# One landing for every transfer in the planner of a hybrid encoder block

## The chip, the cores and the metric

The kernel runs on one core of a Trainium2 chip. The metric is the device time of one execution in microseconds (us). A core has five engines that each work through their own list of instructions in order: TensorE (PE) for matmuls, VectorE (DVE), ScalarE (ACT), GpSimd (POOL) and SyncE (SP), which here only issues transfers. Transfers are also issued by GpSimd and, a few, by ScalarE. All of them are carried by the core's 16 DMA engines.

## The reference

One layer on 256 tokens of width 2048, float32, batch 1:

```python
x = x + 0.5 * swiglu(rms_norm(x, ffn1_norm[l]), ffn1_w_up[l], ffn1_w_down[l])
h = rms_norm(x, mix_norm[l])
proj = h @ w_in[l]
...
merged = g[:, :, 0, :] * (y_a @ w_branch_a[l]) + g[:, :, 1, :] * (y_b @ w_branch_b[l])
x = x + merged @ w_out[l]
x = x + cross_attention(rms_norm(x, xattn_norm[l]), rms_norm(mem, mem_norm[l]),
                        xattn_wq[l], xattn_wkv[l], xattn_wo[l])
x = x + 0.5 * swiglu(rms_norm(x, ffn2_norm[l]), ffn2_w_up[l], ffn2_w_down[l])
return rms_norm(x, final_norm)
```

`swiglu` is `(silu(gate) * up) @ w_down` with an inner width of 5632. `y_a` comes from a gated linear recurrence in chunks, `y_b` from a convolution and a scanned recurrence. Nearly all the work is the product of 256 tokens with weights that are each used once, so each weight is loaded, prepared and multiplied.

## The kernel before

**Stages.** First FFN (about 0 to 660 us), the mixer with its two recurrences, the cross attention (together to about 1745 us), second FFN, final norm. Weights come in pieces of 128x2048 float32, 1 MB each, and TensorE uses one after the other.

**Splitting.** Every product is computed from two parts of each operand: a high part in TensorE's fast float32 form, and what is left. For a weight piece `raw`, ScalarE writes the high part (`h<-raw`) and VectorE the rest (`l<-raw,h`). TensorE then does h times the input's high part (`xh`), h times its rest (`xl`), and l times its high part. So a weight passes through a load, ScalarE, VectorE and TensorE, and each waits for the one before.

**FFNs.** The up projection runs in 11 groups g of 8 pieces. A "fast" piece does a block product with seven products in place of eight; for that VectorE forms differences of weight blocks (`td<-raw`), which are split in turn (`h<-td`, `tl<-td,h`). At the end of a group VectorE and ScalarE take the finished accumulators from PSUM (`ev<-acc`), form the activation, TensorE transposes it (`acc<-vt,ev`), and it is split (`hidop`). Pieces of the down projection (`wd`) come behind each group, two and later four, and their results are added to the tokens (`x<-acc,x`). In the first FFN half of these down pieces are loaded twice: a GpSimd transfer adds the second load to the negated high part (`l<-own`), in place of VectorE's subtraction.

**Made sums.** For 56 pieces of the second FFN the differences are formed ahead, in the middle: GpSimd loads a piece (`made<-wu`), VectorE subtracts four times (`made<-made`), GpSimd stores the result to DRAM (`kept<-made`). In the second FFN SP loads it (`td<-kept`) beside three quarters of the piece itself.

**What sets the order.** The program is not written in the order in which it runs. Every operation is recorded (`record`), priced in microseconds (`price`, L254), and a planner (`arrange`, L291) plays the whole program through: at each step an engine takes, among the operations that are ready, the one that is due first, where due times are counted back from TensorE's. This is done twice. `emit` (L435) then writes each engine's instructions in the order found; so all matmuls, splits and transfers show L465. Semaphores keep the order correct, whatever the true durations are.

For a transfer `price` gives `op.moved`, 2.9 us a MB (5.2 for an accumulating one), and `op.lands`, the time from its last byte to the moment when it can be used. `arrange` lines transfers up behind one another (`dma`), adds the landing to each (`op.end`), and does not issue a further one while more than `BACKLOG` = 3 us are outstanding. `op.lands` enters in two places: in `op.spent`, from which the due times of all earlier operations follow, and in `op.end`, when whatever uses the transfer becomes ready. Buffers (`big`: 9, and 4 more in the FFNs) are given out in the same pass.

Of the kernel before, what the change touches and what calls it, by code (L numbers as in the profile page):

```python
# [176 lines left out]


LAG = {"PE": 0.24, "DVE": 0.15, "ACT": 0.16, "POOL": 0.16, "SP": 0.1}
AHEAD, BACKLOG, STICK = 30, 3, 8  # L180
TABLES = {ACT.Silu, ACT.Sigmoid, ACT.Sqrt, ACT.Exp, ACT.Gelu_apprx_tanh}


class Flow:
# [69 lines left out]
    def price(self, op, method, args, kw, outs):  # L254
        q = op.queue.name
        n = outs[0].cells.size if outs else 0
        if method == "dma_start":
            n = n or args[1].cells.size
            op.moved = n * 512 / 2 ** 20 * (5.2 if "accum_op" in kw else 2.9)
            op.busy = 0.9 if q == "POOL" else 0.06  # L260
            op.lands = 1.9 if q != "POOL" else 3.2 if "accum_op" in kw else 4.6 if op.tiles - {args[0].tile} == set() else 5.8
        elif method == "transpose":
            op.busy += 0.099
        elif q == "PE":
            op.busy += n / 2400 + 0.0137 if not op.turn else 0.021 if n <= 32 else 0.07 + n * 1.05e-3
        elif q == "DVE":
            n = max(n, kw["in_"].cells.size) if method == "tensor_reduce" else n
            per = {"reciprocal": 6.2, "tensor_tensor_scan": 2.2}.get(method, 1.042)
            op.busy = n * per / 1000 + 0.07
        elif q == "ACT":  # L270
            op.busy = n * 0.838e-3 + 0.095 + (0.1 if "accum_out" in kw else 0)
            op.table = args[2] if args[2] in TABLES else None
        else:
            op.busy = 1.0
# [16 lines left out]
    def arrange(self):  # L291
# [2 lines left out]
        ops = self.ops  # L294
        for op in ops:
            op.after = [a for a in getattr(op, "extra", ())]
            op.spent = op.busy + LAG[op.queue.name] + (op.moved + op.lands if op.moved else 0)
        for op in ops:
            op.waits = len(op.deps)
            for d in op.deps:  # L300
# [20 lines left out]
        dma = reached = 0.0  # L321
# [6 lines left out]
        def enter(op):  # L328
            if op.nominal > reached + AHEAD:
                heappush(later[op.queue.name], (op.nominal, op.i, op))  # L330
            else:
                insort(cand[op.queue.name], op, key=lambda o: (o.due, o.i))
# [8 lines left out]
        while events:  # L341
            t, e = heappop(events)
            if free[e] > t + 1e-9:
                continue
            while later[e] and later[e][0][0] <= reached + AHEAD:
                enter(heappop(later[e])[2])
            best, soon = None, 1e18
            for op in cand[e]:
                if best is not None and (not last or best.turn or op.due - STICK > best.due):
                    break  # L350
                if best is not None and not op.turn:
                    continue
                r = op.ready
                if op.moved:
                    r = max(r, dma - BACKLOG)
                if r <= t + 1e-9:
                    for ring in {x.ring for x in op.takes}:
                        fit = ring.fit(op, self)
                        r = max(r, fit[-1][0] if fit else 1e18)
                if r <= t + 1e-9:  # L360
                    best = op
                else:
                    soon = min(soon, r)
            if best is None:
                if soon < 1e17:
                    heappush(events, (soon, e))
                continue
            op = best
            cand[e].remove(op)
            op.start = t  # L370
            sequence.append(op)
            busy = op.busy
            if op.table is not None and op.table != table:
                table = op.table
                busy += 1.3
            if e == "PE":
                busy += 0.1 * (op.turn != last)
                last = op.turn
            free[e] = t + busy
            op.end = t + busy + LAG[e]  # L380
            if op.moved:
                dma = max(dma, t + busy) + op.moved
                op.end = dma + op.lands
            woken = {e}
            if e == "PE" and op.nominal > reached:
                reached = op.nominal
                woken.update(names)
            for ring in {x.ring for x in op.takes}:
                fit = ring.fit(op, self)
                for x in op.takes:  # L390
                    if x.ring is ring:
                        f = fit.pop(0)
                        ring.take(op, f)
                        x.place = f[1]
                        scope = ring.places[f[1]][0].scope
                        if scope is not None:
                            self.opened = max(self.opened, scope)
                            live[scope] += 1
                        if f[2] is not None:
                            for u in f[2].users:  # L400
                                if u is not op:
                                    u.extra.append(op)
                woken.update(names)
            if op.scope is not None:
                live[op.scope] -= 1
            for x in op.tiles:
                x.left -= 1
                x.ends = max(x.ends, op.end)
                if not x.left:
                    x.ring.free.append((x.ends, x.place, x))  # L410
                    if x.ring.places[x.place][0].scope is not None:
                        live[x.ring.places[x.place][0].scope] -= 1
                    woken.update(names)
            for s in op.after:
                kind = s.deps[op]
                if kind is None:
                    r = t
                elif s.queue is op.queue and not op.moved:
                    r = t + busy + (0.1 if kind and e in ("DVE", "ACT") else 0)
                else:  # L420
                    r = op.end
                s.ready = max(s.ready, r)
                s.waits -= 1
                if not s.waits:
                    enter(s)
                    woken.add(s.queue.name)
            for n in woken:
                heappush(events, (max(t, free[n]), n))
            done += 1
# [1231 lines left out]
```

## Time and profile before

| | us |
|---|---|
| median of 3 runs | 2434.31 (2431.85 to 2438.36) |
| profiled execution | 2435.0 |
| its span | 2433.2 |
| TensorE busy | 2412.0 |
| VectorE busy | 2071.1 |
| ScalarE busy | 1417.8 |
| DMA | 662.84 MB, mean 272 GB/s |

The granted TensorE clock is 0.999 of full speed on average. The span is the time from the first to the last instruction in the profile, and the execution's time lies around it. In the rows `out<-in` names the tiles written and read, with their shapes; a wait is booked with what ended it.

### The profile page before, as it was taken

Reading aid. Unit: us, or ns where it says so; the run is one execution under the profiler, and the core shown is the slowest. Engines: PE = TensorE matmul, PEld = TensorE weight load, DVE = VectorE, ACT = ScalarE, POOL = GpSimd, SP = SyncE. Lnnn points to the kernel's source line nnn. Section 1 sums busy time; section 2 is a strip of 40 time slices with the busy share of each in tenths; the row PEclk is TensorE's granted clock in tenths of the full one; section 3 lists DMA queues with packets and bytes.
Section 4 is the critical chain, followed back from the end, with each engine's and each line's share of the span. In section 5 each row is a group of like instructions: output and inputs, shape, how many; then the busy total and the mean of one; then the engine's idle time right before and its main releaser. Section 6 shows DMA issues by size and latency. Waiting matters only on the chain. (4 is left out here: it accounts for less than half of the span.)

```text
span 2433.2 us, 30931 instructions
## 1 busy us (share of the span) xinstructions
PE 2412.0 (99%) x12130; PEld 2008.5 (83%) x12130; DVE 2071.1 (85%) x2232; ACT 1417.8 (58%) x1410; POOL 83.0 (3%) x142
## 2 busy tenths in 40 slices
PE   9999999999999999999999999999999999999998
PEld 8888888888888888888888888888888788888886
DVE  8999999999955778888877877867899999999994
ACT  8556666666654444476434644545676666666663
POOL 0000000000000000000000000000000000000000
PEclk9999999999999999999999999999999999999999
DMA  8567878787835687978988888876898766776783
GB/s 305 187 238 245 266 250 260 258 248 252 279 122 191 255 298 267 355 287 331 345 328 311 336 313 320 318 295 232 329 374 304 260 248 254 253 254 257 259 302 113
DMA packets 98355, 662.84 MB, mean 272 GB/s; under 512 B 10912, under 2 KB 11168, under 8 KB 24992
## 3 DMA queue, kind: packets, MB, share of 16 engines
q1 hardware_dynamic: 77904, 517.11, 56.9%
q0 software_dynamic: 19584, 142.62, 18.0%
q8 instruction: 95, 1.56, 0.2%
q10 hardware_dynamic: 720, 1.13, 0.1%
q14 instruction: 52, 0.43, 0.0%
HBM read 574.83 MB, written 60.82 MB: 261 GB/s over the span
## 5 line engine op out<-in xcount | busy, mean ns | idle before, releaser
L465 ACT ACTIVATE h<-raw 128x2048 fp32r<-128x2048 f32 (+2 forms) x428 | 732.2, 1714 | 508.6 <-PE acc L465 132.6
L465 DVE TENSOR_TENSOR l<-raw,h 128x2048 fp32r<-128x2048 f32 (+2 forms) x428 | 870.7, 2038 | 177.4 <-ACT h L465 80.0
L465 PE MATMUL acc<-h,xh 128*128 128x512 f32 x1244 | 469.9, 390 | 0.9 <-ACT h L465 0.7
L465 PE MATMUL acc<-h,xl 128*128 128x512 f32 x1244 | 449.4, 390 | 0.0
L465 PE MATMUL acc<-h,hidop 128*128 128x512 f32 x1408 | 442.2, 391 | 1.1 <-ACT ev L465 1.1
L465 PE MATMUL acc<-h,ops 128*128 128x512 f32 x1664 | 412.4, 391 | 1.3 <-DVE gate L465 1.2
L465 ACT ACTIVATE h<-td 128x1024 fp32r<-128x1024 f32 (+1 forms) x248 | 307.8, 1249 | 171.2 <-DVE td L465 131.8
L465 PE MATMUL acc<-ops,h 128*128 128x512 f32 x1152 | 388.6, 397 | 1.2 <-ACT h L465 1.2
L465 DVE TENSOR_TENSOR tl<-td,h 128x1024 fp32r<-128x1024 f32 (+1 forms) x248 | 359.2, 1460 | 10.1 <-ACT h L465 7.9
L465 PEld LDWEIGHTS acc<-h,ops 128*128 128x128 f32 x1664 | 310.0, 188 | 65.6 <-DVE gate L465 1.5
L465 PEld LDWEIGHTS acc<-h,hidop 128*128 128x128 f32 x1408 | 262.6, 188 | 56.1 <-ACT ev L465 2.5
L465 PEld LDWEIGHTS acc<-h,xh 128*128 128x128 f32 x1244 | 232.5, 188 | 52.4 <-ACT h L465 3.1
L465 PEld LDWEIGHTS acc<-h,xl 128*128 128x128 f32 x1244 | 233.4, 188 | 48.6
L465 PE MATMUL acc<-ops,l 128*128 128x256 f32 x1152 | 270.1, 281 | 0.0
L465 PE MATMUL acc<-l,hidop 128*128 128x512 f32 x704 | 265.7, 389 | 0.0
L465 PEld LDWEIGHTS acc<-ops,h 128*128 128x128 f32 x1152 | 202.8, 188 | 32.8 <-ACT h L465 1.4
L465 PEld LDWEIGHTS acc<-ops,l 128*128 128x128 f32 x1152 | 211.4, 188 | 19.9
L465 PE MATMUL acc<-l,ops 128*128 128x512 f32 x832 | 222.6, 389 | 0.0
L465 PE MATMUL acc<-tl,xh 128*128 128x512 f32 x608 | 189.3, 392 | 3.3 <-DVE tl L465 3.2
L465 PE MATMUL acc<-l,xh 128*128 128x512 f32 x636 | 187.6, 390 | 0.0
L465 PEld LDWEIGHTS acc<-l,ops 128*128 128x128 f32 x832 | 155.5, 188 | 32.1
L465 DVE TENSOR_TENSOR made<-made 128x512 f32<-128x512 f32 x224 | 153.5, 689 | 13.0 <-DMA made<-wu 8.7
(172 smaller groups left out, 1916.8 us busy)
## 6 DMA issues: line engine op xcount, KB each, us to landing
raw<-wu SPq DMA_DIRECT2D x108, 1024.0 KB, 7.1
raw<-wd SPq DMA_DIRECT2D x72, 1024.0 KB, 6.4
made<-wu POOLq DMA_DIRECT2D x56, 1024.0 KB, 5.9
kept<-made POOLq DMA_DIRECT2D x56, 1024.0 KB, 6.4
td<-kept SPq DMA_DIRECT2D x56, 1024.0 KB, 6.7
raw<-wu SPq DMA_DIRECT2D x56, 768.0 KB, 5.6
raw<-win SPq DMA_DIRECT2D x40, 1024.0 KB, 4.9
raw<-wg SPq DMA_DIRECT2D x32, 1024.0 KB, 6.8
```

Of the source, the lines that this page charges most:

```text
L465: getattr(op.queue.real, method)(*map(real, args), **{k: real(v) for k, v in kw.items()})
```

## The change

In place of four landings, one for SP's and ScalarE's queues (1.9), and three for GpSimd's (3.2 for an accumulating load, 4.6 for a load, 5.8 for a store), the planner uses 3.5 us for every transfer.

```diff
-AHEAD, BACKLOG, STICK = 30, 3, 8
+AHEAD, BACKLOG, STICK, LANDS = 30, 3, 8, 3.5
...
             op.moved = n * 512 / 2 ** 20 * (5.2 if "accum_op" in kw else 2.9)
             op.busy = 0.9 if q == "POOL" else 0.06
-            op.lands = 1.9 if q != "POOL" else 3.2 if "accum_op" in kw else 4.6 if op.tiles - {args[0].tile} == set() else 5.8
...
-            op.spent = op.busy + LAG[op.queue.name] + (op.moved + op.lands if op.moved else 0)
+            op.spent = op.busy + LAG[op.queue.name] + (op.moved + LANDS if op.moved else 0)
...
                 dma = max(dma, t + busy) + op.moved
-                op.end = dma + op.lands
+                op.end = dma + LANDS
```

No operation is added or removed. The order changes on all five engines; three places of it follow. The line is L465 before and L464 after, since one line of the program is gone.

VectorE at the end of a group of the first FFN (the fourth or a later group; `td` are differences of up weights, `tl` their rest parts, `l<-raw,h` of 128x2048 those of down weights, `ev` the accumulators taken from PSUM). Before:

```order
L465 TENSOR_TENSOR td<-raw 128x1024
L465 TENSOR_TENSOR l<-raw,h 128x1536
L465 TENSOR_TENSOR tl<-td,h 128x1024
L465 TENSOR_TENSOR td<-raw,td 128x512
L465 TENSOR_TENSOR tl<-td,h 128x1024
L465 TENSOR_TENSOR td<-raw,td 128x512
L465 TENSOR_TENSOR l<-raw,h 128x2048
L465 TENSOR_TENSOR tl<-td,h 128x1024
L465 TENSOR_TENSOR l<-raw,h 128x2048
L465 TENSOR_TENSOR ev<-acc,ev 128x512 x5
```

After, from the same td on:

```order
L464 TENSOR_TENSOR td<-raw 128x1024
L464 TENSOR_TENSOR tl<-td,h 128x1024
L464 TENSOR_TENSOR td<-raw,td 128x512
L464 TENSOR_TENSOR l<-raw,h 128x1536
L464 TENSOR_TENSOR td<-raw,td 128x512
L464 TENSOR_TENSOR tl<-td,h 128x1024 x2
L464 TENSOR_TENSOR ev<-acc,ev 128x512 x2
L464 TENSOR_TENSOR l<-raw,h 128x2048
L464 TENSOR_TENSOR ev<-acc,ev 128x512 x2
L464 TENSOR_TENSOR l<-raw,h 128x2048
L464 TENSOR_TENSOR ev<-acc,ev 128x512
```

The last tl of the group moves ahead of the first split of down weights, and two of the five ev move ahead of it too.

VectorE in the middle of a late group of the second FFN, where a `tl` of 128x2048 belongs to a piece whose differences were stored before and one of 128x1024 to half of a piece whose differences are formed here. Before:

```order
L465 TENSOR_TENSOR l<-raw,h 128x1536
L465 TENSOR_TENSOR tl<-td,h 128x2048
L465 TENSOR_TENSOR tl<-td,h 128x1024
L465 TENSOR_TENSOR tl<-td,h 128x2048
L465 TENSOR_TENSOR l<-raw,h 128x1536
```

After:

```order
L464 TENSOR_TENSOR l<-raw,h 128x1536
L464 TENSOR_TENSOR tl<-td,h 128x1024
L464 TENSOR_TENSOR tl<-td,h 128x2048
L464 TENSOR_TENSOR l<-raw,h 128x1536
L464 TENSOR_TENSOR tl<-td,h 128x2048
```

The half `tl` moves ahead of the first whole one, and the second whole one behind a split of `raw`.

ScalarE at the end of a late group of the second FFN, where `h<-raw` of 128x2048 splits down weights and `ev<-acc` takes the first accumulator. Before:

```order
L465 ACTIVATE h<-td 128x1024
L465 ACTIVATE h<-raw 128x2048 x3
L465 ACTIVATE ev<-acc 128x512
L465 ACTIVATE h<-raw 128x2048
L465 ACTIVATE h<-raw 128x1536
L465 ACTIVATE ev<-ev,rtok 128x512
```

After:

```order
L464 ACTIVATE h<-td 128x1024
L464 ACTIVATE h<-raw 128x2048 x2
L464 ACTIVATE ev<-acc 128x512
L464 ACTIVATE h<-raw 128x2048 x2
L464 ACTIVATE ev<-ev,rtok 128x512
L464 ACTIVATE h<-raw 128x1536
```

`ev<-acc` moves ahead of the third split of down weights.

## The prediction

> **What bounds the kernel now.** I read the page's first part, then TensorE's own waits, then busy time by stretch, and last the places where TensorE stands still. The page's busy times and its span:
>
> ```profile
> span 2433.2 us, 30931 instructions
> PE 2412.0 (99%) x12130; PEld 2008.5 (83%) x12130; DVE 2071.1 (85%) x2232; ACT 1417.8 (58%) x1410; POOL 83.0 (3%) x142
> ```
>
> TensorE (PE) works 2412.0 of 2433.2 us. The 21.2 us that are left are all that any order can win. Where they lie, from TensorE's waits over the whole span, and the end of the chain of waits:
>
> ```profile
> PE acc L465 <- DVE tl L465: 3.2, 6, 0.9
> PE acc L465 <- ACT h L465: 1.9, 3, 1.2
> PE acc L465 <- ACT xg L465: 1.3, 1, 1.3
> PE acc L465 <- DVE gate L465: 1.2, 1, 1.2
> PE acc L465 <- ACT ev L465: 1.1, 2, 0.6
> PE warm L465 <- DVE ones L465: 1.1, 1, 1.1
> PE acc L465 <- DVE sum L465: 0.4, 1, 0.4
> PE acc L465 <- DVE hidop L465: 0.4, 1, 0.4
> PE acc L465 <- ACT vf L465: 0.3, 1, 0.3
> 2337.19 85.97 PE acc L465 x382
> ```
>
> The columns are the total, the number of waits and the longest. They sum to 10.9 us; 1.1 of it is the start, so 9.8 us are waits inside. The last matmul ends at 2337.19 + 85.97 = 2423.2, and the remaining 10.0 us are the final norm and the stores, which no order of loads shortens. No TensorE wait names a DMA: weights are late for ScalarE and VectorE, hardly ever for TensorE.
>
> The second engine decides how much disorder is forgiven. Busy time by stretch (TensorE, its weight loads, VectorE (DVE), ScalarE (ACT), GpSimd; clock; DMA share; GB/s), the first of the span, two of the first FFN, one of the middle and two of the second FFN:
>
> ```profile
> 0.00:60.00 60.00, 58.95 (x268) 50.01 (x269) 50.31 (x79) 51.50 (x86) 0.20 (x4) 1.00 0.81 304
> 240.00:300.00 60.00, 60.00 (x270) 49.72 (x269) 57.04 (x59) 41.86 (x34) 2.57 (x3) 1.00 0.80 255
> 300.00:360.00 60.00, 60.00 (x271) 49.76 (x270) 56.29 (x58) 40.38 (x33) 2.61 (x3) 1.00 0.79 249
> 1140.00:1200.00 60.00, 60.00 (x266) 49.71 (x265) 47.90 (x54) 28.86 (x30) 4.82 (x9) 1.00 0.97 350
> 1980.00:2040.00 60.00, 60.00 (x269) 49.43 (x268) 59.37 (x52) 37.38 (x30) 0.00 (x0) 1.00 0.67 254
> 2160.00:2220.00 60.00, 58.83 (x263) 48.14 (x262) 56.98 (x50) 35.89 (x29) 0.00 (x0) 1.00 0.69 250
> ```
>
> In both FFNs VectorE has only 0.6 to 3.7 us to spare in 60; in the middle it has 12. So an order that makes VectorE stand still costs time in the FFNs first.
>
> **Which landing is nearer.** The change moves no work; it gives the planner other landings. For a transfer of 1 MB it adds 2.9 us of moving to the landing (5.2 where it accumulates): before 4.8 for the SP queue, 7.5 for a GpSimd load, 8.7 for a store to DRAM, 8.4 for an accumulating load; after it 6.4, 6.4, 6.4 and 8.7. The page has the medians from issue to landing (last column):
>
> ```profile
> raw<-wu SPq DMA_DIRECT2D x108, 1024.0 KB, 7.1
> raw<-wd SPq DMA_DIRECT2D x72, 1024.0 KB, 6.4
> made<-wu POOLq DMA_DIRECT2D x56, 1024.0 KB, 5.9
> kept<-made POOLq DMA_DIRECT2D x56, 1024.0 KB, 6.4
> l<-own POOLq DMA_DIRECT2D x24, 1024.0 KB, 8.0
> ```
>
> The new numbers are nearer to the median on the first four rows; on the last, the accumulating load, the plan goes from 0.4 over to 0.7 over. Part of a measured landing is queueing, which the planner counts apart, so this speaks for the change without proving it. The answers on tile raw and on tile made give the spread:
>
> ```profile
> DMA to landing us min/median/max: 4.0/6.2/13.6
> DMA to landing us min/median/max: 4.1/5.9/10.9
> ```
>
> An undisturbed load takes 4.0 to 4.1, less than either plan; a disturbed one 10.9 to 13.6, more than both.
>
> **The change part by part.** TensorE's matmuls are the same ones, so its 2412.0 us stay; the start (1.1) and the end (10.0) stay too: in the new order the last token half's result waits for the first half's scaling, but the first half also ends 11 matmuls ahead of the last instead of 8, and I take nought, between -0.5 and 0.5. What is left are the waits, stage by stage.
>
> *Second FFN.* TensorE's wait for tl from 1800 on, then chain pieces and VectorE's rows around one such wait and one for ev:
>
> ```profile
> PE acc L465 <- DVE tl L465: 1.6, 3, 0.6
> 2171.35 1.92 ACT h L465
> 2173.27 0.48 ACT ev L465
> 2173.80 39.74 PE acc L465 x178
> 2214.56 121.83 PE acc L465 x542
> 2209.22 1.76 DVE L465 TENSOR_TENSOR l<-raw,h 128x1536 fp32r<-128x1536 f32 x1
> 2211.07 5.63 DVE L465 TENSOR_TENSOR tl<-td,h 128x2048 fp32r<-128x2048 f32 x3
> ```
>
> At 2173 the copy of a finished accumulator (ev) stands behind a third split of down weights on ScalarE, and TensorE needs the bank: 0.6 us. The new order has the copy behind two splits: with that the wait goes. At 2213.5 (2173.80 + 39.74) TensorE needs the half tl (128x1024) of one piece, but VectorE does the whole tl (2048) of the next piece first. The new order turns the two round: 0.6 gone as well. Both patterns come in several groups. The gain is bounded by the 2.7 us of such waits (1.6 for tl, 1.1 for ev, whose two waits both lie here) and by nought, if VectorE's little spare time lets another piece be late; I take 2.0, nearer the upper end, as the rows show the very pairs that are turned round. What replaces it: the third down split is late next, on ScalarE, which has 22 us in 60 to spare.
>
> *First FFN.* TensorE waits here 3.2 - 1.6 = 1.6 us for tl and 0.4 for hidop, 2.0 in all. The end of a group, VectorE and then TensorE:
>
> ```profile
> 257.43 2.29 DVE L465 TENSOR_TENSOR l<-raw,h 128x2048 fp32r<-128x2048 f32 x1
> 259.63 1.22 DVE L465 TENSOR_TENSOR tl<-td,h 128x1024 fp32r<-128x1024 f32 x1
> 261.10 2.29 DVE L465 TENSOR_TENSOR l<-raw,h 128x2048 fp32r<-128x2048 f32 x1 [0.25 <-ACT h L465]
> 263.31 3.33 DVE L465 TENSOR_TENSOR ev<-acc,ev 128x512 f32<-128x512 f32 x5
> 261.15 0.61 PE L465 MATMUL acc<-tl,xh 128*128 128x512 f32 x2
> ```
>
> VectorE ends the last tl at 260.8, and TensorE takes it at 261.15. The new order puts this tl ahead of the down split: 2.2 us earlier, about 258.6. But then two ev come ahead of both down splits, and they read accumulators that TensorE finishes at about 261.4. So VectorE, a strict queue, would stand there for 261.4 - 258.6 = 2.8 us, with two down splits, five more ev, and then the next group's td and l behind it. TensorE needs the first of those splits only after the down entry it is working on (24 matmuls, some 5.4 us), so the place itself is hidden; what counts is whether VectorE catches up in a group. A group is 267 such matmuls and 8 transposes, by the 121.83 us for 542 above about 61.4 us. VectorE's work in it is 56.7 of 60, so 57.9; after the new wait it must go once round the group, and the 0.9 us of last matmuls follow: 58.8 and what it waits on the way. Its waits for loads in the first FFN (60 to 660):
>
> ```profile
> DVE td L465 <- DMA raw<-wu: 17.2, 9, 3.1
> DVE l L465 <- ACT h L465: 7.3, 12, 2.3
> ```
>
> That is 24.5 us in ten groups, 2.5 each: 58.8 + 2.5 = 61.3 against 61.4. The group is just balanced; the eight groups of this pattern cost between nought and, at 0.6 us each, 5 us. Being 2.8 us behind also eats up part of these waits, so I take 1.5, and 1.0 gained of the 2.0 by the earlier tl. At the start, loads and splits change places with the sums of squares; the row of the first 60 us shows TensorE idle for 1.05, its start alone, so all of that is hidden by now. I leave it at nought; one split that comes late there would cost no more than its own length, about 2 us.
>
> *Middle.* Its TensorE waits are 1.3 + 1.2 + 1.2 + 0.4 + 0.3 = 4.4 us at most, and that is the most to gain. GpSimd's made loads are now expected 1.1 us earlier and its stores 2.3 us earlier, so VectorE's differences and SP's next loads are put closer behind them. The row of VectorE's waits so far:
>
> ```profile
> DVE made L465 <- DMA made<-wu: 8.7, 7, 2.2
> ```
>
> If each of the 56 loads cost VectorE 1.1 us more, that is 62 us over some 900, under 5 in 60 where 12 are free. TensorE sees it only where the next weight is nearly due. From -4.4 to +10 (two loads at the worst landing, 10.9 against a planned 6.4, 4.5 us each); I take +2.0, since waits of a new order fall at new places.
>
> **The sum.** 2433.2 - 2.0 (second FFN) - 1.0 + 1.5 (first FFN) + 2.0 (middle) + 0 (start, end) = 2433.7, half a microsecond over this execution's span. It took 2435.0, 1.8 beyond its span, and the three runs have 2431.9 to 2438.4 with a median of 2434.3; on that median the forecast is 2434.8.
>
> **Rivals.** *Faster (R1):* landings near the measured ones remove most waits. For it speaks that the two turned pairs are right; against it that only 9.8 us exist, and 0.3% of the time, 7.3 us (about what a measurement of this kernel can tell from no change), is three quarters of them. It gives 2434.3 - 8.5 = 2425.8.
>
> *Slower through VectorE in the FFNs (R2):* the plan now expects SP's loads later than undisturbed ones come, so it puts work on results of TensorE ahead of splits that could have gone first. If the 2.8 us at ev come on top of the present waits in place of them, the group is 57.9 + 2.8 + 3.5 (all present idleness) = 64.2, 2.8 over, and eight groups cost 22 us; with half of it, 2445. It decides from the point at which VectorE's waits pass 2.6 us a group, and they stand at 2.5. Against it: VectorE that is late finds its loads landed.
> The Trainium skill (DMA: Bandwidth & Descriptors, Anatomy of one DMA) speaks for R2: it puts a GpSimd transfer at 2.0 us fixed plus its bytes over 436 GB/s, and the fixed part is mostly the receipt of the last write. For 1 MB that would be an estimate of 4.4 us, with which the old 4.8 for SP is the better number and the new one is 2 us late. The shortest landings, 4.0 and 4.1, agree with it; the medians, 5.9 and 6.2, do not.
>
> *Slower in the middle (R3):* loads and stores of GpSimd land later than the shortened plan, where the DMA engines are 97% busy; three such events of 4.5 us make 2448. Against it: no TensorE wait there names a DMA so far.
>
> That the change does nothing is ruled out by the new order itself, which differs on all five engines.
>
> **How the numbers follow.** Forecast (2427 to 2441.6) 0.55, R1 0.07, R2 0.21, R3 0.17. The forecast's own range is all within 0.3%; R2 and R3 go over it. So faster 0.07, same 0.55, slower 0.38. The range that leaves out no more than 2 in 10: below it is 2427, where R1 begins; above it takes R2 at half price and R3, to 2450, and leaves out R2 at its full price.
>
> **What would show it.** TensorE's busy time within 2 us of 2412. In the second FFN no wait for ev and fewer for tl. In the first FFN a VectorE idle of up to 2.8 us before the first ev of each group, named after TensorE, with TensorE idle under 1 us a group; if it is idle by 2 or 3, R2 is right. In 660 to 1740, TensorE waits under 6 us and none above 2; a wait of 4 or more behind GpSimd's loads is R3. The forecast is wrong if TensorE's waits inside sum to over 17 us or under 2.5.

## The result and the profile after

| | before | after |
|---|---|---|
| median of 16 runs each | 2433.11 (2429.07 to 2438.36) | 2428.14 (2425.87 to 2431.28) |
| profiled execution | 2435.0 | 2425.98 |
| its span | 2433.2 | 2424.2 |

The ratio is 0.9979, 95% interval 0.9971 to 0.9987: the change makes the kernel 5.0 us (0.2%) faster. The profiled execution of before lies 1.9 us above its median and that of after 2.2 us below, so the two traces differ by 9.0 us where the medians differ by 5.0. What is read from one pair of traces is to be taken with some 4 us of doubt, and for that reason the stages are compared over many kernels below.

The page of after, its span and busy times:

```profile
span 2424.2 us, 30937 instructions
PE 2408.9 (99%) x12130; PEld 2008.3 (83%) x12130; DVE 2066.3 (85%) x2232; ACT 1420.8 (59%) x1411; POOL 83.0 (3%) x142
```

TensorE issues the same 12130 matmuls, and yet its busy time has fallen by 3.1 us, from 2412.0. Its own waits over the whole span (total, number, longest):

```profile
PE acc L464 <- DMA l<-own: 1.9, 3, 1.0
PE acc L464 <- DVE p L464: 1.1, 2, 0.6
PE warm L464 <- DVE ones L464: 1.1, 1, 1.1
PE acc L464 <- DVE merge L464: 0.5, 1, 0.5
PE acc L464 <- DVE sum L464: 0.4, 1, 0.4
PE acc L464 <- ACT h L464: 0.3, 1, 0.3
PE acc L464 <- DVE l L464: 0.2, 1, 0.2
PE acc L464 <- DVE ev L464: 0.2, 1, 0.2
PE acc L464 <- DVE hidop L464: 0.2, 1, 0.2
```

Without the start these sum to 4.8 us, where before had 9.8. The waits for tl, for xg and for ScalarE's ev are gone. The largest of the new ones is for an accumulating load (`l<-own`), where before no wait named a DMA.

VectorE's three largest waits in the first FFN (60 to 660 us):

```profile
DVE ev L464 <- PE acc L464: 21.0, 10, 2.7
DVE td L464 <- DMA l<-own: 5.0, 7, 1.5
DVE td L464 <- DMA raw<-wu: 3.7, 6, 1.1
```

VectorE now stands 21.0 us at the first ev of ten groups, and its wait for up weights has shrunk from 17.2 to 3.7: it is late, and finds its loads landed. All its waits in this stretch sum to 30.0 us, before to 31.0.

To put the gain into stages I compare when TensorE starts the same transposes in the two traces: the last ones of the first FFN, the first of the second FFN, the last of the second FFN. Before:

```profile
648.43 1.03 PE L465 MATMUL acc<-vt,ev 128*128 128x128 f32 x8
1793.42 0.60 PE L465 MATMUL acc<-vt,ev 128*128 128x128 f32 x4
2374.05 1.03 PE L465 MATMUL acc<-vt,ev 128*128 128x128 f32 x8
```

After:

```profile
646.96 1.03 PE L464 MATMUL acc<-vt,ev 128*128 128x128 f32 x8
1790.33 0.60 PE L464 MATMUL acc<-vt,ev 128*128 128x128 f32 x4
2366.11 1.03 PE L464 MATMUL acc<-vt,ev 128*128 128x128 f32 x8
```

The differences are 1.5, 3.1 and 7.9 us. So the first FFN gives 1.5, the middle 1.6, the second FFN 4.9, and 1.1 is left for the end (9.0 of span less 7.9). More than half lies in the second FFN.

One pair of traces misleads here on the first FFN. Three of the kernels below have exactly after's order in that stage, and their traces lose 2.0, 2.6 and 2.6 us there against before, where after's own gains 1.5. With their mean, a loss of 2.4, the 9.0 us become 5.1, which is what the medians say.

### The profile page after: what moved, and what is told of

Same layout as the page of the kernel before. It is cut to its first block, busy times and chain, and to the rows that moved or that the text cites. A ratio compares the mean times of both kernels' runs of the same rounds, so it can differ in the third digit from the quotient of the medians.

```text
span 2424.2 us, 30937 instructions
## 1 busy us (share of the span) xinstructions
PE 2408.9 (99%) x12130; PEld 2008.3 (83%) x12130; DVE 2066.3 (85%) x2232; ACT 1420.8 (59%) x1411; POOL 83.0 (3%) x142
## 5 line engine op out<-in xcount | busy, mean ns | idle before, releaser
L464 DVE TENSOR_TENSOR l<-raw,h 128x2048 fp32r<-128x2048 f32 (+2 forms) x428 | 870.9, 2039 | 163.6 <-PE acc L464 65.4
L464 ACT ACTIVATE h<-raw 128x2048 fp32r<-128x2048 f32 (+2 forms) x428 | 730.7, 1713 | 449.0 <-DVE l L464 182.0
L464 PE MATMUL acc<-h,xh 128*128 128x512 f32 x1244 | 471.1, 390 | 0.8 <-ACT h L464 0.3
L464 PE MATMUL acc<-h,xl 128*128 128x512 f32 x1244 | 449.3, 389 | 0.0
L464 PE MATMUL acc<-h,hidop 128*128 128x512 f32 x1408 | 440.0, 390 | 0.0
L464 ACT ACTIVATE h<-td 128x1024 fp32r<-128x1024 f32 (+1 forms) x248 | 308.1, 1251 | 199.7 <-DVE td L464 180.8
L464 PE MATMUL acc<-h,ops 128*128 128x512 f32 x1664 | 411.8, 391 | 0.0
L464 PE MATMUL acc<-ops,h 128*128 128x512 f32 x1152 | 391.8, 397 | 0.1
L464 DVE TENSOR_TENSOR tl<-td,h 128x1024 fp32r<-128x1024 f32 (+1 forms) x248 | 360.8, 1463 | 2.4 <-ACT h L464 0.7
L464 PEld LDWEIGHTS acc<-h,ops 128*128 128x128 f32 x1664 | 310.1, 188 | 63.7
L464 PEld LDWEIGHTS acc<-h,hidop 128*128 128x128 f32 x1408 | 262.9, 188 | 53.5
L464 PEld LDWEIGHTS acc<-h,xh 128*128 128x128 f32 x1244 | 233.1, 188 | 51.4 <-ACT h L464 2.0
L464 PEld LDWEIGHTS acc<-h,xl 128*128 128x128 f32 x1244 | 233.5, 188 | 48.3
L464 PE MATMUL acc<-ops,l 128*128 128x256 f32 x1152 | 273.5, 281 | 0.0
L464 PE MATMUL acc<-l,hidop 128*128 128x512 f32 x704 | 264.3, 390 | 2.0 <-DMA l<-own 1.9
L464 PEld LDWEIGHTS acc<-ops,h 128*128 128x128 f32 x1152 | 202.4, 188 | 32.9 <-DVE ops L464 0.9
L464 PEld LDWEIGHTS acc<-ops,l 128*128 128x128 f32 x1152 | 212.6, 188 | 19.8
L464 PE MATMUL acc<-l,ops 128*128 128x512 f32 x832 | 223.0, 390 | 0.0
L464 PE MATMUL acc<-tl,xh 128*128 128x512 f32 x608 | 187.6, 390 | 0.0
L464 PE MATMUL acc<-l,xh 128*128 128x512 f32 x636 | 186.2, 390 | 0.2 <-DVE l L464 0.2
L464 PEld LDWEIGHTS acc<-l,ops 128*128 128x128 f32 x832 | 155.5, 188 | 32.4 <-DVE l L464 0.4
L464 DVE TENSOR_TENSOR made<-made 128x512 f32<-128x512 f32 x224 | 153.4, 688 | 20.3 <-DMA made<-wu 16.7
```

The lines of the kernel that those rows point to most:

```text
L464: getattr(op.queue.real, method)(*map(real, args), **{k: real(v) for k, v in kw.items()})
```

## The experiments

Each kernel was timed against before on the same chip; before's medians beside them are 2432.69 to 2433.15. In the table "landings" are those of SP, GpSimd's load, its store and its accumulating load; before has 1.9, 4.6, 5.8, 3.2. The stage columns are us gained on the trace of before, worked out as above from the same three transposes; they come from one trace each, and all_but_second's is its slowest execution, 2442.81, 4.7 us above its median.

| kernel | landings | median | ratio (95%) | first FFN | middle | second FFN |
|---|---|---|---|---|---|---|
| after | 3.5 for all | 2428.14 | 0.9979 (0.9971, 0.9987) | 1.5 | 1.6 | 4.9 |
| second_only | as after from the second FFN's loads on | 2426.97 | 0.9972 (0.9960, 0.9983) | 0.3 | 0.4 | 4.9 |
| all_but_second | as after up to there | 2438.09 | 1.0020 (1.0011, 1.0029) | -2.0 | -1.5 | -4.7 |
| sp_only | 3.5, 4.6, 5.8, 3.2 | 2423.87 | 0.9957 (0.9944, 0.9971) | 5.1 | 1.2 | 4.9 |
| gpsimd_only | 1.9, 3.5, 3.5, 3.5 | 2435.03 | 1.0015 (1.0001, 1.0029) | 4.8 | -5.3 | 1.0 |
| old_lag | as before | 2428.43 | 0.9978 (0.9970, 0.9987) | 1.1 | 3.7 | 0.6 |
| sp_lag | as sp_only | 2420.96 | 0.9953 (0.9941, 0.9965) | 5.4 | 3.0 | 4.9 |
| sp_4_5 | 4.5, 4.6, 5.8, 3.2 | 2423.38 | 0.9963 (0.9951, 0.9975) | 3.6 | 2.2 | 4.4 |
| sp_2_7 | 2.7, 4.6, 5.8, 3.2 | 2423.11 | 0.9961 (0.9950, 0.9973) | 5.0 | 2.4 | 5.3 |
| after_lag | as after | 2427.52 | 0.9975 (0.9966, 0.9984) | -2.6 | 2.2 | 4.9 |
| accum_3_2 | 3.5, 3.5, 3.5, 3.2 | 2424.24 | 0.9962 (0.9950, 0.9974) | 5.5 | -0.7 | 4.9 |
| store_cut | 3.5, 4.6, 3.5, 3.5 | 2430.32 | 0.9986 (0.9977, 0.9994) | -2.6 | 2.3 | 4.9 |
| lands_5_0 | 5.0 for all | 2424.33 | 0.9963 (0.9952, 0.9974) | 5.6 | 2.4 | 3.4 |

These are not thirteen independent orders. Compared engine by engine, by the names and shapes of the rows, after, all_but_second, after_lag and store_cut have one and the same order in the first FFN; sp_only, sp_lag and accum_3_2 share another, and second_only has before's. In the second FFN VectorE, ScalarE and the transfers have one order in after, second_only, sp_only, accum_3_2 and store_cut, from which after_lag and sp_lag differ in 18 rows; all_but_second has before's, and gpsimd_only and old_lag differ from that in fewer than ten. Traces of one order are repeats, and show how far a stage's value can be trusted.

### Where: one part of the program alone

```diff
 op.lands = 1.9 if q != "POOL" else 3.2 if "accum_op" in kw else ...
+op.lands = 3.5 if self.second else op.lands        # second_only
+op.lands = 3.5 if not self.second else op.lands    # all_but_second
```

`self.second` is set just ahead of the recording of the second FFN.

> 3.5 us for the transfers recorded in the second FFN, the old landings elsewhere. Theory A (the gain lies in the second FFN, where the accumulator copy and the half tl come earlier): 3 to 5 us under the kernel before, ratio 0.998 to 0.9988, TensorE's waits for tl and ev from 1740 on gone, first FFN and middle waits as before (about 7). Theory B (the gain is spread over all stages): 1 to 2 us under. Theory C (it is the chance of one order): within 1 us of the kernel before, or over it.

> 3.5 us for the transfers recorded in the first FFN and the middle, the old landings in the second FFN. Theory A: within 1.5 us of the kernel before (ratio 0.9993 to 1.0003), waits for tl and ev from 1740 on still about 2.7. Theory B: 3 us under it. Theory C: anything from 5 under to 5 over.

The second FFN alone makes the kernel 5.8 us faster than before (2426.97 against 2432.76), no less than the whole change. TensorE's waits of second_only from 1740 us on are those of after, nearly to the tenth:

```profile
PE acc L466 <- ACT h L466: 0.3, 1, 0.3
PE acc L466 <- DVE ev L466: 0.3, 1, 0.3
PE acc L466 <- DVE l L466: 0.2, 1, 0.2
```

Its first 1793 us, whose order on VectorE, ScalarE and the transfers differs from before's in fewer than 20 rows, agree with before's trace to 0.7 us. Other repeats agree less: the four traces of after's first FFN end it 4.1 us apart (646.96 to 651.07).

The other kernel was expected within 1.5 us of before by theory A, and is 5.3 us slower (2438.09 against 2432.76). In its trace the first FFN and the middle with one landing cost 3.5 us, and the second FFN is 4.7 us slower than in before, although its order there is before's own. TensorE's waits for ScalarE's ev have grown from 1.1 to 3.5 us, while that for xg is what it was:

```profile
PE acc L466 <- ACT ev L466: 3.5, 3, 2.2
PE acc L466 <- ACT xg L466: 1.3, 1, 1.3
```

The longest of them, ScalarE and then TensorE, with the row of busy times by stretch behind it (the columns as in the prediction, the granted clock third from the end):

```profile
2299.70 1.91 ACT L466 ACTIVATE h<-raw 128x2048 fp32r<-128x2048 f32 x1 [2.12 <-PE acc L466]
2301.52 0.58 ACT L466 ACTIVATE ev<-acc 128x512 f32<-128x512 f32 x1
2302.15 2.50 PE L466 MATMUL acc<-h,hidop 128*128 128x512 f32 x5 [2.22 <-ACT ev L466]
2302.10:2305.70 3.60, 3.55 (x9) 2.83 (x10) 3.60 (x3) 2.99 (x2) 0.00 (x0) 0.53 0.46 196
```

ScalarE's split of down weights waits 2.12 us for TensorE, the copy of the accumulator stands behind that split, and TensorE waits 2.22 us for the copy. It is the pair that the change turns round. Then TensorE's granted clock is 0.5 for 3.4 us, and matmuls of 128x512 start 0.43 us apart in place of 0.227: an estimated 1.7 us more, half of the 3.4. Together this is some 3.9 of the 4.7 us, from one event in the slowest of eleven executions. Between the first and the last transposes of the second FFN the old order, or one within ten rows of it, took 579.6 to 585.3 us in four traces (before 580.6), and after's, or one within 18 rows of it, 575.7 to 575.8 in seven. So the order with the copy ahead is faster, and in these traces it also repeats better.

### Which queue

```diff
-op.lands = 1.9 if q != "POOL" else 3.2 if "accum_op" in kw else ...
+op.lands = 3.5 if q != "POOL" else 3.2 if "accum_op" in kw else ...   # sp_only
+op.lands = 1.9 if q != "POOL" else 3.5                                # gpsimd_only
```

> 3.5 us for SP's transfers, the three old landings for GpSimd's. Theory A, by which the later landing of SP's loads puts the copies and the half tl ahead: nearly the whole gain, 4 to 5 us under the kernel before. If the shorter GpSimd landings carry it: within 1 us of before. Prediction's R2 (late landings for SP make VectorE stand at ev): 2 us or more over.

> 3.5 us for GpSimd's transfers, the old 1.9 for SP's. Theory A: within 1 us of the kernel before, with TensorE's waits of 2.7 in the second FFN still there. If the GpSimd landings carry the gain: 3 to 5 us under. Prediction's R3 (the middle suffers from shorter GpSimd landings): 2 us or more over, with new waits between 800 and 1740.

The later landing of SP's loads alone wins 8.9 us, more than the change. GpSimd's alone loses 2.3 us, by an interval that hardly excludes 1. Its trace shows the third rival of the prediction at work, at one place in the middle (VectorE, ScalarE, TensorE; in brackets the idle time ahead and what ended it):

```profile
1357.52 2.15 DVE L465 TENSOR_TENSOR made<-made 128x512 f32<-128x512 f32 x3 [2.77 <-DMA made<-wu]
1360.52 1.28 DVE L465 TENSOR_TENSOR x<-acc,x 128x512 f32<-128x512 f32 x2
1361.26 0.33 PE L465 MATMUL acc<-vt,x 128*128 128x128 f32 x1 [2.86 <-DVE x L465]
```

VectorE stands 2.77 us for a load that GpSimd issued; the token sums (`x<-acc,x`) are queued behind it, and TensorE, which transposes them, loses 2.86 us. The wait is named after VectorE, though a DMA is its cause. Here too the granted clock is 0.5 for 3.4 us afterwards (from 1362.9), an estimated 1.7 us more, so that this place makes some 4.6 of the 5.3 us that the middle loses. After has no wait of TensorE for x.

### Is it the number, or any other order?

```diff
-LAG = {"PE": 0.24, "DVE": 0.15, "ACT": 0.16, "POOL": 0.16, "SP": 0.1}
+LAG = {"PE": 0.24, "DVE": 0.16, "ACT": 0.16, "POOL": 0.16, "SP": 0.1}
```

This moves a planner's number for VectorE by 0.01 us, and with it the order: on VectorE, ScalarE and the transfers' queues about 40 rows of before's first FFN change places, 160 of the middle, and fewer than ten of the second FFN. old_lag has before's landings, sp_lag those of sp_only, after_lag those of after. sp_2_7 and sp_4_5 are sp_only with other numbers for SP.

> The landings of before (SP 1.9, GpSimd 4.6, 5.8 and 3.2), and one other number of the planner moved by a hair: VectorE's lag 0.15 to 0.16 us. It makes an order that differs in thousands of rows but with no better knowledge of landings. Theory N (the nearer landing of the SP queue is what wins): the time stays within 0.1% of before, some 2.5 us, and TensorE's waits inside stay near 10 us. Theory C (an order that is thrown anew wins or loses some us by chance, whatever number was changed): the time moves by 3 us or more, either way, as much as the change's own 5.

> SP at 3.5 and GpSimd's three old landings, as in the kernel that took 2423.9, with VectorE's lag at 0.16 in place of 0.15. Theory N: the gain is there again, 2422 to 2427 us beside a before of about 2433, and TensorE's waits inside are under 4 us. Theory C: the 9 us were a lucky order; this one lies anywhere from 2424 to 2436, likeliest near before.

> SP at 2.7, half way between 1.9 and 3.5, GpSimd's old landings. Theory N: half of the 9 us that 3.5 won, 2426 to 2431, with waits for tl and ev partly left. Theory C: anywhere from 2424 to 2438. A threshold (the pairs of splits are turned round as soon as the planner sees the load late by 0.5 us): as good as 3.5, 2422 to 2426.

> SP at 4.5 and GpSimd's old landings. Issue to landing is 7.1 in the median for the up weights and 6.4 for the down weights, less 2.9 of moving 4.2 and 3.5, so 4.5 errs on the late side by 0.3 to 1.0 where 1.9 erred on the early side by 1.6 to 2.3. Theory N: 2422 to 2428, with waits inside under 5 us. Theory C: no relation to the number, 2424 to 2438. Too late a plan (the second rival of the prediction, VectorE standing behind TensorE's results): above 2433, with waits for ev and tl in the FFNs.

> The changed kernel, one landing of 3.5 for all, with VectorE's lag at 0.16 in place of 0.15: another order from the same landings. Theory S (later SP landings win about 9, shortened GpSimd landings give 4 of it back): 2426 to 2430. Theory C (what separates the changed kernel's 2428 from the 2421 to 2424 of the four orders with GpSimd's old landings is the chance of one order): 2420 to 2425 is as likely as 2426 to 2432.

The control is the run that matters most: 0.01 us in a number that has nothing to do with transfers wins 4.3 us; its 0.9978 stands beside the change's 0.9979. The change's median alone proves nothing about landings. The middle of old_lag, with all the old landings, gains 3.7 us, and the first FFN of gpsimd_only, with SP's old one, 4.8. So a gain of 5 us is within what a new order brings by chance.

More can be said of the second FFN. It gains 3.4 to 5.3 us in each of ten kernels in which SP's landing there is 2.7 or more, and -4.7, 0, 0.6 and 1.0 in the four with 1.9 (before among them). But seven of the ten have after's order there, or one within 18 rows of it, and the four with 1.9 have before's, or one within ten: it is four orders with a later landing (after's, sp_2_7's, sp_4_5's, lands_5_0's) against a single one with 1.9. The control hardly moves this stage, so it does not tell what another order with 1.9 would gain there. What is shown is that the change's second FFN, put in alone, gives the gain (second_only), that the waits of the turned pairs are gone, and that all four later orders have it; that a later landing wins in any order is likely, and not shown.

All four kernels with SP later and GpSimd's old landings are at 2421 to 2424, below every run of before (2428.37 at the lowest in the set). Against old_lag, the other order with old landings, they are 4.6 to 7.5 us faster. 2.7 does as well as 4.5: as far as these orders show, what is needed is that the planner expects these loads later than 1.9, not a certain value. Half the gain at 2.7, as nearness would have it, did not come.

The prediction weighed a rule of the Trainium skill (DMA: Bandwidth & Descriptors, Anatomy of one DMA) by which 1 MB lands after an estimated 4.4 us, so that the old plan of 4.8 would be right for SP and a later one an error. The Trainium skill gives this rule for GpSimd's transfers. A plan of 5.6 (2.7 + 2.9) to 7.4 (4.5 + 2.9) is the better one in these runs, and the medians in before's trace are 6.4 and 7.1.

sp_lag is the fastest kernel of the set, 2420.96 us, 0.9953 of before with an interval clear of the change's. Its page and its waits:

```profile
span 2418.9 us, 30928 instructions
PE 2406.1 (99%) x12130; PEld 2008.0 (83%) x12130; DVE 2067.9 (85%) x2232; ACT 1427.7 (59%) x1414; POOL 83.2 (3%) x142
```

```profile
PE acc L465 <- DVE l L465: 1.1, 2, 0.8
PE warm L465 <- DVE ones L465: 1.1, 1, 1.1
PE acc L465 <- DVE ev L465: 0.8, 2, 0.5
PE acc L465 <- ACT h L465: 0.5, 2, 0.3
```

Its waits inside sum to 2.4 us, 7.4 less than before's 9.8, but its span is 14.3 us shorter.

### What the change gives back in the first FFN

The change's order has 1.5 us there in its own trace and -2.0, -2.6 and -2.6 in the three repeats; sp_only's has 5.1. Three kernels look for the cause, each the change with one thing put elsewhere:

```diff
+op.lands = 3.2 if "accum_op" in kw else 3.5                                   # accum_3_2
+op.lands = (3.5 if q != "POOL" or "accum_op" in kw
+            else 4.6 if op.tiles - {args[0].tile} == set() else 3.5)          # store_cut
-AHEAD, BACKLOG, STICK, LANDS = 30, 3, 8, 3.5
+AHEAD, BACKLOG, STICK, LANDS = 30, 3, 8, 5.0                                  # lands_5_0
```

> The changed kernel with only the accumulating load put back to 3.2 (SP, GpSimd's loads and stores at 3.5). If the later plan for the accumulating load (0.3 us) made the three waits of TensorE for it in the first FFN, these go, the first FFN ends 3 to 4 us earlier against before (5 gained by then in place of 1.5), and the time is 2424 to 2426. If they come from GpSimd's other two landings, the waits for the accumulating load stay and the time is that of the changed kernel, 2427 to 2430.

> The changed kernel with only GpSimd's plain load put back to 4.6 (its store at 3.5, the accumulating load at 3.5, SP at 3.5). If the plan that expects the differenced weights back too early is what costs in the middle (the third rival), the middle, from the end of the first FFN to the start of the second, gains 1 to 3 us as with all three old landings, in place of 0.4, and the time is 2424 to 2427. If the shortened store costs it, it stays at 2427 to 2430.

> The changed kernel with 5.0 in place of 3.5 for every transfer. Medians from issue to landing less the planned moving are 3.0 to 4.2 for loads and stores and 2.8 for the accumulating load, so 5.0 is 0.8 to 2.2 late for all. Theory near (the landing nearest to the measured one wins): slower than the changed kernel, 2429 to 2440. Theory late (a plan that expects transfers late keeps a reserve and loses nothing by it): 2420 to 2426, as the four orders with SP later and GpSimd's old landings. Chance of one order: either.

It is the accumulating load, and 0.3 us of its plan: with 3.2 the kernel takes 2424.24, 3.9 less than after. The planner then arrives at sp_only's order of the first FFN, and this stage ends at 642.9 to 643.4 us in the three traces of that order, against 647.0 to 651.1 in the four of after's. TensorE's waits for `l<-own`, 1.9 to 5.5 us in all, exist in after, after_lag, store_cut and all_but_second, which share that order, and in no other kernel. VectorE's stand in the first FFN of accum_3_2 is gone as well:

```profile
DVE td L465 <- DMA raw<-wu: 2.8, 4, 1.3
DVE ev L465 <- PE acc L465: 2.5, 2, 1.3
```

How the loss comes about can be seen at the end of one group. After (start, duration, engine; ScalarE's `ev<-ev,rtok` scales what VectorE has taken from PSUM):

```profile
320.66 1.42 DVE L464 TENSOR_TENSOR ev<-acc,ev 128x512 f32<-128x512 f32 x2 [2.49 <-PE acc L464]
324.91 0.72 ACT L464 ACTIVATE ev<-ev,rtok 128x512 f32<-128x512 f32 x1 [2.40 <-DVE ev L464]
325.54 1.90 ACT L464 ACTIVATE l<-own 128x2048 fp32r<-128x2048 f32 x1
327.84 0.87 POOL L464 DMA_DIRECT2D l<-own  x1 [20.36 <-DVE l L464]
340.07 1.23 DVE L464 TENSOR_TENSOR td<-raw 128x1024 f32<-128x1024 f32 x1 [1.47 <-DMA l<-own]
340.09 0.50 PE L464 MATMUL acc<-l,hidop 128*128 128x512 f32 x1 [0.97 <-DMA l<-own]
```

The same place with 3.2:

```profile
322.29 1.91 ACT L465 ACTIVATE l<-own 128x2048 fp32r<-128x2048 f32 x1
324.60 0.87 POOL L465 DMA_DIRECT2D l<-own  x1 [20.01 <-ACT l L465]
326.94 0.72 ACT L465 ACTIVATE ev<-ev,rtok 128x512 f32<-128x512 f32 x1 [0.94 <-DVE ev L465]
340.37 0.84 PE L465 MATMUL acc<-l,hidop 128*128 128x512 f32 x3
```

In after VectorE stands 2.49 us at ev. ScalarE's scaling waits for it, and in ScalarE's queue the negated copy (`l<-own`) is behind the scaling. So the copy ends and GpSimd issues the accumulating load 3.2 us later (327.84 against 324.60), it lands 12.2 us after that, and TensorE is stopped. With 3.2 the copy is ahead of the scaling, and the load, though it takes 11.8 us, lands in time. The stand alone does no harm: sp_2_7 stands 2.19 us in the same place, but has the copy ahead, and gains 5.0 in the first FFN:

```profile
320.54 0.69 DVE L465 TENSOR_TENSOR ev<-acc,ev 128x512 f32<-128x512 f32 x1 [2.19 <-PE acc L465]
322.12 1.92 ACT L465 ACTIVATE l<-own 128x2048 fp32r<-128x2048 f32 x1 [0.17 <-DMA own<-wd]
324.45 0.87 POOL L465 DMA_DIRECT2D l<-own  x1 [17.71 <-ACT l L465]
326.86 0.72 ACT L465 ACTIVATE ev<-ev,rtok 128x512 f32<-128x512 f32 x1 [1.02 <-DVE ev L465]
```

It takes both, the late issue and the long landing. Before issues the same load as late as after, but there it lands 7.3 us later, and TensorE does not wait:

```profile
327.47 0.87 POOL L465 DMA_DIRECT2D l<-own  x1 [18.12 <-DVE l L465]
```

Putting GpSimd's plain load back (store_cut) helped nothing: 2430.32, with after's order in the first FFN. (Its expectation speaks of 0.4 us for the middle; that is second_only's figure, and after's is 1.6.) And 5.0 for everything, later than all medians, takes 2424.33, 3.8 less than 3.5: in this one order a late plan costs nothing, and nearness to the measured landing is not what wins. Why the planner puts the copy behind the scaling with 3.5, and ahead of it with 3.2 and with 5.0, is open; it isn't a matter of "later is better" for this number.

The middle moves between -5.3 and 3.7 us with no order by any landing. Three kernels whose middles differ in fewer than 30 rows (after, accum_3_2, all_but_second; VectorE, ScalarE and the transfers) have 1.6, -0.7 and -1.5, so one trace is good to some 1.5 us there. That GpSimd's shorter landings cost there, as sp_only against accum_3_2 (1.2 and -0.7) and gpsimd_only suggest, is not borne out by store_cut and lands_5_0 (2.3 and 2.4), and stays open.

## Why the prediction failed

The forecast was 2434.8, no change with a lean to slower; the kernel takes 2428.1. This is inside the range and within the 0.3% named there, but on the other side, and the interval of the ratio excludes 1.

**"TensorE's 2412.0 us stay" and "9.8 us are waits inside".** This is the step that failed first, since all bounds on a gain hung on it. Consecutive matmuls of 128x512 start 0.227 us apart, while a row lasts 0.39: a wait of up to 0.16 us after each is booked as busy, and of any longer one so much is hidden. Between the first and the last transposes of the second FFN quoted above, the starts that are further than 0.227 apart exceed it by some 8.2 us before (3.1 shown as idle, 5.1 hidden) and by some 3.8 after (0.6 and 3.2); where one draws the line for "further" moves a sum by up to 0.8, and their difference from 4.4 to 4.8. So 4.4 us or more of the 4.9 are waits, and two fifths to a half of these never stood in the list of waits. The clock has no part in it: in both traces it is 1.00 until after the last matmul.

**Second FFN, -2.0.** Right in mechanism, wrong in size: -4.9, beyond the bound of 2.7, and 5.8 by the medians of second_only. No wait for tl is left, ScalarE's ev is gone, and VectorE's ev is one of 0.2 us. The bound came from the shown waits of two kinds alone. By the medians this term makes 3.8 of the 5.5 us by which the sum was off: second_only alone has 5.8, and the whole change 5.0, so its other stages together came out some 0.8 slower, where 2.5 slower was forecast.

**First FFN, -1.0 + 1.5.** The stand of VectorE was foreseen at 2.8 us; the row has 2.7 at most and ten of them. It came in place of its other waits, not on top (30.0 us of waits in all against 31.0), which is where the second rival fell. The 24.5 us that the prediction took for those waits leave out three rows of before's list:

```profile
DVE tl L465 <- ACT h L465: 4.5, 4, 1.1
DVE x L465 <- PE acc L465: 1.7, 4, 0.9
DVE l L465 <- issue: 0.3, 1, 0.3
```

With these 6.5 us its 61.3 against 61.4 a group becomes 61.9, and the balance is no safe sign either way. The reckoning asked only whether VectorE catches up, and it does. What was late next stood on another queue, behind ScalarE: the accumulating load. That part cost 3.9 us by accum_3_2's median, against the 1.5 put down for another reason; and without that loss the stage gains 5.1 to 5.5, where 1.0 was booked for the earlier tl. The stage came out at -1.5 in after's trace and at 2.0 to 2.6 in the three repeats of its order, where 0.5 was forecast.

**Middle, +2.0.** In after's trace it is -1.6, in the two kernels with nearly its order 0.7 and 1.5: nought, within what one trace can tell, and inside the bounds of -4.4 and 10. The reason given, that new waits fall at new places, is right about the size and can't give the sign. The third rival's chain exists, in gpsimd_only and not in after.

**Start and end, 0 within 0.5.** The end is 1.1 us shorter in this pair of traces.

**The shortest landings.** The 4.0 us that the prediction calls an undisturbed load belong to a piece of 256 KB, and the 4.1 to a store. In before's trace loads of 1 MB took 4.6 us at least on SP's queue and 4.9 on GpSimd's, so all of them took longer than the 4.4 us estimated there, and the agreement that the prediction saw was with other transfers.

**The sum against the median.** 1.1 us were added to the span, on the median of three runs. Against the median of 16 runs before's execution was 1.9 too long.

**The rivals.** R1 had the direction, and was 2.3 us too fast: the waits of before go, and the new one for `l<-own` takes part of it back. Its reason, that the landings are near the measured ones, is not borne out, since 2.7 for SP and 5.0 for all do as well. What was missing was the case that the order itself is a draw: old_lag shows that a change of no meaning moves this kernel by 4.3 us.

## What to carry over

Where a planner's number sets the order of the whole program, test it with several numbers and with a meaningless one, by stage, before believing a single median: here the change's 5 us could be chance, while SP's later landing won 9 to 12 us in each of four kernels (4.6 to 7.5 against the control). Ask also which stages of two kernels really have different orders: where the order is the same, a second trace is a repeat and not a second proof. In these kernels it paid to plan loads later than the shortest ones land. And where an engine is made to stand, look at what stands behind whoever waits for it on the next queue, not only at its own work.

## What the runs showed of the hardware

TensorE's shown waits understate what is lost: sp_lag's busy time is 5.9 us below before's for the same 12130 matmuls, since a wait of up to 0.16 us between two pipelined matmuls is counted as busy. A longer wait cost more than itself in two traces: after waits of TensorE of 2.22 us (all_but_second) and 2.86 us (gpsimd_only) its granted clock was 0.5 for 3.4 us, while the longest wait without this was 1.83 us (gpsimd_only). An accumulating load of 1 MB took 12.2 us from issue to landing in a busy stretch, where the answer on its tile in after gives:

```profile
DMA to landing us min/median/max: 4.9/9.0/12.2
```
